# A decoder layer on one Trainium2 core: norms of heads taken for two tiles of tokens together, values third among the projections, and a filler's pace set by its present steps

## The chip, the cores and the metric

The kernel is one program on one core of a Trainium2 chip. The metric is device time in microseconds (us). Before the change three runs took 2496.92, 2497.53 and 2503.78 us; their median is 2497.53.

The core has a matrix engine (TensorE, PE in the profile, with its weight loads listed as PEld), a vector engine (VectorE, DVE), a scalar engine (ScalarE, ACT), and queues of transfers. In this kernel every transfer is issued by SyncE (SP), in the order of its instructions. Matrix products land in PSUM, which has eight banks of 128 x 512 numbers; a tile there may take one bank or two.

## The reference, cut to what matters

One layer of a decoder on 1024 tokens of width 1024: a half-step feed-forward, a mixing part with three kinds of attention, and a second half-step. The change lies in the mixing part:

```
u  = rmsnorm(h)
(fq, fk, fv, ff, dq, dk, dv, iq, ik, iw, mq, g) = split(u @ w_in)
fq, fk = rmsnorm per head (8 heads of 64);  o_a = forgetting attention(fq, fk, fv, log_sigmoid(ff))
dq     = rope(rmsnorm per head (8 heads of 64)); iq, ik = rope(...)
o_b    = attention of dq over the 256 keys with the highest sum_h iw_h * relu(iq_h . ik)
mq     = rmsnorm per head (4 heads of 128);  o_c = attention of mq into 256 memory tokens
h      = h + (sum_i sigmoid(g_i) * (o_i @ w_branch_i)) @ w_out
```

## The kernel before, in words

Tokens are taken in eight tiles of 128. Each product of float32 numbers is done in three passes: operands are split into a high and a low part (`wH`, `wL` for weights; the cast to `wH` is on ScalarE, the difference `wL` on VectorE), so that 8 slices of the inner size 1024 make 24 matmuls for one tile of 128 tokens and 512 columns.

The stages follow one another: first feed-forward up to about 706 us of the span, norms and narrow projections, then the *projections* up to about 1118 us, the *heads* up to about 1697 us (four memory heads, eight forgetting heads, eight sparse heads, two at a time), the *last branch* up to 1757 us, the output product up to 1840 us, and the second feed-forward.

**Projections.** Six blocks of 512 columns, listed in `blocks` (line 1675): memory queries, index queries, forget keys, forget queries, values, sparse queries. A block has eight steps, one for each tile: `Block.step` (line 353) takes one PSUM bank (`bank("tm")`), issues the 24 matmuls, asks for the next block's weights in its last step, and hands the tile to a `consume` function. For keys and queries this is a norm by head (`head_norm`, line 857): a square on ScalarE (`hsq<-tm`), a sum by head on VectorE (`hv<-hsq`), nine small steps of VectorE for the inverse root (`rsqrt_mean`: `hv`, `rs_y`, `rs_a`), and a multiply that reads the bank again (`hsq<-tm,rs_y`). Then `turn` transposes the tile on TensorE (`turn<-ident,hsq`), splits it (`th`, `tl`), and the halves are stored. For sparse queries a rotation on VectorE stands between norm and `turn`. Values (`fox_values`) are only split and stored; their tile has the tag `iqs`, with two buffers.

Index queries go further: for tiles 2 to 7 the queries are loaded back (also under the tag `iqs`, two buffers), and for each of eight heads TensorE computes scores against the keys (`isc`, into a two-bank tile `banks2("isc")`), ScalarE takes the relu in place, and VectorE adds them up (`acc`). A background chain then looks for the 256th highest score of each token by a binary search (`junk` on ScalarE, `sk` and `sn` on VectorE).

While projections run, PSUM is cut into four single banks (tag `a`, used by `bank`) and two double ones (tag `b`, used by `banks2`).

**What sets the order.** The work is written as chains (generators), and a planner, `_Flow.run`, steps them at build time: it charges estimated costs to each engine, and picks the first of the `width` oldest chains that is ready by TensorE's clock, else a step of a filler (12 matmuls of the gate products `gate`), else it waits. The framework afterwards reorders instructions on each engine by its own estimates, so the order on an engine is finer than the planner's steps.

**Heads and their filler.** During the heads the filler (`fill`, line 1697) has the remaining gate steps, then 16 steps of one branch product (memory), four steps that wait for forgetting heads, and 17 of another. `pace` (line 1754) lets it run while its count of steps is below a share of `left` that grows with the heads' steps, plus 4, and below `left` − 6. `left` is gate steps remaining + 40. After the heads the last branch (sparse, `last_branch`) starts, once the filler is done; its first operands are the heads' outputs (`o_s`) and the weights `in_w_branch`.

Of the kernel before, what the change touches and what calls it, by code (L numbers as in the profile page):

```python
# [9 lines left out]
F32 = mybir.dt.float32  # L10
# [9 lines left out]
P = 128  # L20
# [11 lines left out]
C_FQ, C_FK, C_FV, C_FF = 0, 512, 1024, 1536  # L32
C_DQ, C_DK, C_IQ, C_IK, C_MQ, C_G = 1544, 2056, 2184, 2696, 2768, 3280
# [122 lines left out]
def trunk_layer_kernel(  # L156
# [6 lines left out]
    fl = _Flow(nc)  # L163
    T, A, V = fl.T, fl.A, fl.V
    chain = _Chain
# [3 lines left out]
    def plain(ap):  # L169
        return ap.bitcast(F32) if ap.dtype == F32R else ap  # L170
# [4 lines left out]
    def store(o, i):  # L175
        nc.sync.dma_start(plain(o), plain(i))
# [19 lines left out]
    def pool(name, bufs=1, **kw):  # L196
        return Pool(name, bufs, **kw)
# [18 lines left out]
    def bank(name="bank"):  # L216
        return banks["pool"].tile([P, 512], F32, tag="a", name=name, bufs=banks["single"])
# [4 lines left out]
    def banks2(name="banks2"):  # L222
        return banks["pool"].tile([P, 1024], F32, tag="b", name=name, bufs=2)
# [6 lines left out]
    def split(high, low, v):  # L230
        A.copy(high, v)
        V.tensor_sub(low, v, high.bitcast(F32))
# [101 lines left out]
    def mm3(pt, terms, first, last, onto=False):  # L334
        n = len(terms)
        for i, (a, b) in enumerate(terms):
            T.matmul(pt, a, b, start=first and i == 0, stop=last and i == n - 1, skip_group_check=onto)

    class Block:
# [13 lines left out]
        def step(self, u, t, consume, after=None):  # L353
            self.fetch()
            if fl.clk["PE"] < self.ready[0]:
                yield self.ready[0]
            if after is not None:
                after.fetch(self.bufs - len(self.srcs))
            pt = self.out(t) if self.out else bank("tm")
            kper = 1024 // self.ncols  # L360
            for k in range(NK):
                wh, wl = self.ws[k // kper]
                wh, wl = wh[:, k % kper], wl[:, k % kper]
                a, b = [u.at(w, k, t * P, P) for w in range(2)]
                mm3(pt[:, :self.ncols], [(a, wh), (a, wl), (b, wh)], k == 0, k == NK - 1)
                if after is not None and k % kper == kper - 1:
                    after.fetch(self.bufs - len(self.srcs) + k // kper + 1)
            yield from consume(t, pt)

    def col_srcs(w, c0, ncols):  # L370
        kper = 1024 // ncols
# [5 lines left out]
    def block_chains(blocks, u, nt, deps=None, after=None):  # L377
        cs = []
        for i, (b, consume) in enumerate(blocks):
            nxt = blocks[i + 1][0] if i + 1 < len(blocks) else after  # L380
            order = getattr(consume, "order", range(getattr(consume, "first", 0), nt))
            for t in order:
                cs.append(chain(b.step(u, t, consume, nxt if t == order[-1] else None),
                                deps[t] if deps and i == 0 else getattr(consume, "deps", ())))
        return cs

# [81 lines left out]
    class FeedForward:  # L468
# [62 lines left out]
        def product(self, pt, j, n, start):  # L531
            sh, sl = self.jobs[j][n]
            th, tl = self.c.high[RIGHT[n]], self.c.low[RIGHT[n]]
            for k in range(4):
                mm3(pt, [(sh[:, k], th[:, k]), (sh[:, k], tl[:, k]), (sl[:, k], th[:, k])],
                    start and k == 0, k == 3, not start)
# [64 lines left out]
        def first_half(self, beside=None):  # L601
# [10 lines left out]
            def prep(g, *js):  # L612
                for j in js:
                    if g in (1, 2):
                        self.prep_sums(j, g - 1)
                    self.prep_split(j, g)

            step()
            c.split(T2, 2)
            prep(1, 0, 1)  # L620
# [212 lines left out]
    def scratch(name, shape):  # L833
        return dram.tile(shape, F32, name=name)
# [3 lines left out]
    fq_s = scratch("fq_s", [2, 8, 64, S])  # L838
    fk_s = scratch("fk_s", [2, 8, 64, S])
    dq_s = scratch("dq_s", [2, 8, 64, S])  # L840
# [3 lines left out]
    mq_s = scratch("mq_s", [2, 4, P, S])  # L844
# [10 lines left out]


    def head_norm(tp, pt, nh, sq=None):
        hd = 512 // nh
        if sq is None:
            sq = tp.tile([P, 512], F32, tag="hx", name="hsq", bufs=4)  # L860
        A.activation(sq, pt, AF.Square)
        v = tp.tile([P, nh], F32, tag="hv", name="hv", bufs=3)
        V.reduce_sum(v, sq.rearrange("p (h d) -> p h d", h=nh), axis=AX.X)
        y = rsqrt_mean(tp, v, hd)
        V.tensor_tensor(
            sq.rearrange("p (h d) -> p h d", h=nh), pt.rearrange("p (h d) -> p h d", h=nh),
            y.unsqueeze(2).to_broadcast([P, nh, hd]), op=OP.mult,
        )
        return sq


    def turn(tp, xn, scale=None):
        pt = bank("turn")
        for j in range(4):
            T.transpose(pt[:, j * P:(j + 1) * P], xn[:, j * P:(j + 1) * P], ident)
        th = tp.tile([P, 4, P], F32R, tag="th", name="th", bufs=2)
        tl = tp.tile([P, 4, P], F32R, tag="tl", name="tl", bufs=2)
        thf, tlf = th.rearrange("p a t -> p (a t)"), tl.rearrange("p a t -> p (a t)")
        if scale is None:
            split(thf, tlf, pt)  # L880
        else:
            A.activation(thf, pt, AF.Identity, scale=scale)
            V.scalar_tensor_tensor(tlf, pt, scale, thf.bitcast(F32), op0=OP.mult, op1=OP.subtract)
        return th, tl

    def store_pairs(dst, t, parts):
        for i, th in enumerate(parts):
            store(dst[i].rearrange("(a b) d t -> (b d) a t", b=2)[:, :, t * P:(t + 1) * P], th)
# [115 lines left out]
    def rotate(tp, o, xv, cv, sv0, sv1, n, op1=OP.add):  # L1004
        t2 = tp.tile([P, n, 2, 32], F32, tag="hx", name="rot2", bufs=4)
        V.tensor_tensor(o, xv, cv, op=OP.mult)
        V.tensor_tensor(t2[:, :, 0], xv[:, :, 1], sv0, op=OP.mult)
        V.tensor_tensor(t2[:, :, 1], xv[:, :, 0], sv1, op=OP.mult)
        if op1 == OP.add:
            V.tensor_add(o, o, t2)  # L1010
        else:
            V.tensor_sub(o[:, :, 0], o[:, :, 0], t2[:, :, 0])
            V.tensor_add(o[:, :, 1], o[:, :, 1], t2[:, :, 1])
# [397 lines left out]
    gfx, gfk, gmx, gmk = [vec.tile([P, 1], F32, name=n) for n in ("gfx", "gfk", "gmx", "gmk")]  # L1411
# [79 lines left out]
    up, u = mixing["up"], mixing["u"]  # L1491
# [5 lines left out]
    gates_f = chain(gates.work())  # L1497
    norms = [chain(to_mix(t)) for t in range(4, NT)]
    nch = block_chains([(nb, narrow)], u, NT, [[]] * 4 + [[c] for c in norms])
    order = norms[:1] + nch[:2] + norms[1:2] + nch[2:3] + norms[2:3] + nch[3:4] + norms[3:]  # L1500
# [8 lines left out]
    tp = pool("proj")  # L1509
    tmp = pool("narrow")  # L1510
    cs, sn = tp.tile([P, NT, 32], F32, name="rope_cos"), tp.tile([P, NT, 32], F32, name="rope_sin")
    cgq, sgq = [tp.tile([P, NT, 2, 32], F32, name=n) for n in ("cgq", "sgq")]
# [3 lines left out]
    mk_block = lambda c0: Block(blk, col_srcs(w_in, c0, 512), 512, 5)  # L1516
    mq_block = mk_block(C_MQ)
# [126 lines left out]
    index_queries.first, index_queries.deps = 2, [prep]  # L1644
    sel_c = chain(selection())

    def normed(dst, nh, scale):
        def consume(t, pt):
            xn = head_norm(tp, pt, nh)
            yield  # L1650
            parts = turn(tp, xn, scale)
            if nh == 8:
                store_pairs(dst, t, parts)
            else:
                for i, w in enumerate(parts):
                    store(dst[i].rearrange("h d t -> d h t")[:, :, t * P:(t + 1) * P], w)
        return consume

    def sparse_queries(t, pt):
        xn = head_norm(tp, pt, 8)  # L1660
        o = tp.tile([P, 512], F32, tag="hx", name="hsq", bufs=4)
        bc = lambda a, s: a.unsqueeze(1).to_broadcast(s)
        rotate(tp, o.rearrange("p (h a d) -> p h a d", h=8, a=2), xn.rearrange("p (h a d) -> p h a d", h=8, a=2),
               bc(cgq[:, t], [P, 8, 2, 32]), bc(sgq[:, t, 0], [P, 8, 32]), bc(sgq[:, t, 1], [P, 8, 32]), 8)
        yield
        store_pairs(dq_s, t, turn(tp, o))

    def fox_values(t, pt):
        vt = tp.tile([P, 8, P], F32R, tag="iqs", name="iqs", bufs=2)
# [2 lines left out]
        return  # L1672
        yield

    blocks = [(mq_block, normed(mq_s, 4, gmx[:, 0:1])), (mk_block(C_IQ), index_queries),
              (mk_block(C_FK), normed(fk_s, 8, None)), (mk_block(C_FQ), normed(fq_s, 8, gfx[:, 0:1])),
              (mk_block(C_FV), fox_values), (mk_block(C_DQ), sparse_queries)]
    chains = block_chains(blocks, u, NT)
    fl.run(chains[:2] + [prep] + chains[2:], width=5, filler=gates_f, background=sel_c, margin=0.5)
    tp.release()  # L1680
# [6 lines left out]
    tp = pool("att")  # L1687
# [60 lines left out]
    sparses = [chain(sparse_chain(i)) for i in range(8)]  # L1748
    fill_c = chain(fill())
    heads = mems + foxes + sparses  # L1750
    left = 2 * 24 * 2 - gates_f.n + 40
    total = 4 * 10 + 8 * 16 + 8 * 20

    def pace():
# [27 lines left out]
    hp = pool("h2", side="right")  # L1782
    h = [hp.tile([P, D], F32, name=f"h2_{t}") for t in range(NT)]
    for t in range(NT):
        load(h[t], h_s[t])
    tp = pool("norm3", side="right")
# [34 lines left out]
    blocks = [(Block(None, col_srcs(w_out, i * 512, 512), 512, 4), f) for i, f in enumerate((residual, normed_rows))]  # L1821
# [51 lines left out]
```

## Time and profile before

| | |
|---|---|
| median of three runs | 2497.53 us |
| the profiled execution's own time | 2504.25 us |
| its span | 2502.2 us |
| granted TensorE clock, mean over the span | 0.984 |
| bytes moved | 352.15 MB, 141 GB/s |

The profile is one execution; times within it are from the start of the span. Each row of the views has an engine, an operation, and its tiles as out<-in, by the names used above. "Idle before" is the time for which the engine stood still just ahead of these instructions, with what released it. Matmul ends are modelled, so a matmul's own duration (about 0.39 us) is longer than the distance between the starts of two. The number after the clock is the share of the DMA engines that was busy.

### The profile page before, as it was taken

What the parts mean: (1) busy time and instruction counts of PE and PEld (TensorE: products, weight loads), DVE (VectorE), ACT (ScalarE), POOL (GpSimd) and SP (SyncE); (2) the same over time, 40 slices, a digit from 0 to 9 for tenths busy, and PEclk for the clock granted to TensorE, in tenths of its full rate; (3) what the DMA queues carried; (4) which work ended last, traced back from release to release, by engine and by line L of the source; (5) the groups of instructions that cost most, each with busy time, mean ns of one, the idle gap of its engine ahead of it and who ended that gap; (6) DMA issues with size and microseconds to landing.
All of it is one profiled execution on the core that took longest, in us unless ns stands there. A gap on an engine that the chain in (4) does not pass through costs nothing.

```text
span 2502.2 us, 31494 instructions
## 1 busy us (share of the span) xinstructions
PE 2412.6 (96%) x11532; PEld 1995.0 (80%) x11532; DVE 1617.9 (65%) x3162; ACT 1149.1 (46%) x1918; POOL 2.2 (0%) x40
## 2 busy tenths in 40 slices
PE   6999999999999999989999999998999999999999
PEld 5888888888788877777787888887877888888887
DVE  7755555478767588685564556777367555554885
ACT  6443333343443376768864555543144333333332
POOL 0000000000000000000000000000000000000000
PEclk8999999999999999999999999999999999999999
DMA  4333322484445534544554546667413222225643
GB/s 136 117 103 110 101 92 73 146 316 142 135 131 146 163 100 137 164 147 137 153 162 135 154 133 195 194 200 238 145 64 93 85 93 76 84 93 194 260 151 131
DMA packets 300922, 352.15 MB, mean 141 GB/s; under 512 B 19896, under 2 KB 202840, under 8 KB 300768
## 3 DMA queue, kind: packets, MB, share of 16 engines
q1 hardware_dynamic: 300768, 350.15, 43.7%
q8 instruction: 90, 1.47, 0.2%
q14 instruction: 64, 0.52, 0.1%
HBM read 255.51 MB, written 93.54 MB: 139 GB/s over the span
## 4 chain that ended last, share of the span: by engine, by line
PE 74%; DVE 12%; ACT 7%; DMA 4%; issue 3%; SPq 0%; ACTq 0%; DVEq 0%
PE gx L51 19%; PE gy L51 14%; PE dx L51 8%; PE gate L51 7%; PE tm L51 7%; PE dy L51 6%; PE br L51 4%; ACT junk L51 3%; PE po L51 2%; PE sp L51 2%; DVE wL L51 2%; PE pT L51 2%; DMA wS<-in_ffn_w_down 1%; PE nar L51 1%; ACT ns L51 1%
## 5 line engine op out<-in xcount | busy, mean ns | idle before, releaser
L51 ACT CAST wH<-wS 128x1024 fp32r<-128x1024 f32 (+1 forms) x218 | 204.6, 944 | 260.7 <-PE gy L51 78.0
L51 PE MATMUL tm<-wH,u 128*128 128x512 f32 x992 | 319.5, 396 | 3.4 <-ACT wH L51 3.4
L51 DVE TENSOR_TENSOR wL<-wS,wH 128x1024 fp32r<-128x1024 f32 (+1 forms) x218 | 236.2, 1089 | 101.1 <-ACT wH L51 98.8
L51 PE MATMUL gate<-u,wH 128*128 128x512 f32 x768 | 248.9, 401 | 0.0
L51 PE MATMUL gx<-th,wH 128*128 128x512 f32 x704 | 223.2, 399 | 10.3 <-ACT wH L51 6.2
L51 PE MATMUL gy<-th,wH 128*128 128x512 f32 x704 | 220.9, 395 | 5.3 <-DVE th L51 3.5
L51 PEld LDWEIGHTS tm<-wH,u 128*128 128x128 f32 x992 | 187.4, 189 | 42.0 <-ACT wH L51 4.6
L51 PE MATMUL gx<-raw,wH 128*128 128x512 f32 x704 | 216.9, 389 | 0.4 <-DVE gu L51 0.4
L51 PE MATMUL tm<-wL,u 128*128 128x512 f32 x496 | 195.1, 393 | 1.0 <-DVE wL L51 0.8
L51 ACT ACTIVATE junk<-wk,sn 128x384 bf16<-128x384 f32 (+5 forms) x186 | 164.3, 883 | 67.4 <-DVE sn L51 59.0
L51 PEld LDWEIGHTS gx<-th,wH 128*128 128x128 f32 x704 | 135.0, 193 | 40.6 <-ACT wH L51 7.4
L51 ACT CAST wH<-S 128x1024 fp32r<-128x1024 f32 x88 | 92.2, 1051 | 157.9 <-PE gy L51 149.9
L51 PEld LDWEIGHTS gy<-th,wH 128*128 128x128 f32 x704 | 133.6, 190 | 34.7 <-DVE th L51 4.4
L51 PEld LDWEIGHTS gate<-u,wH 128*128 128x128 f32 x768 | 140.3, 191 | 24.8 <-DVE u L51 0.2
L51 DVE TENSOR_TENSOR pl<-pT,ph 128x512 fp32r<-128x512 f32 (+1 forms) x176 | 110.1, 639 | 74.5 <-ACT ph L51 73.1
L51 DVE TENSOR_TENSOR wL<-S,wH 128x1024 fp32r<-128x1024 f32 x88 | 107.4, 1223 | 75.1 <-ACT wH L51 75.1
L51 DVE TENSOR_TENSOR gu<-gu,gy 128x512 f32<-128x512 f32 x88 | 60.3, 686 | 147.0 <-PE gy L51 104.1
L51 PEld LDWEIGHTS gx<-raw,wH 128*128 128x128 f32 x704 | 132.0, 188 | 28.2 <-DVE gu L51 0.8
L51 PE MATMUL gate<-u,wL 128*128 128x512 f32 x384 | 151.7, 395 | 0.0
L51 PE MATMUL dx<-wH 128*128 128x512 f32 x352 | 138.4, 393 | 2.7 <-DVE rows L51 2.6
L51 PE MATMUL gx<-th,wL 128*128 128x512 f32 x352 | 139.1, 396 | 0.6 <-DVE wL L51 0.5
L51 PE MATMUL gy<-th,wL 128*128 128x512 f32 x352 | 138.8, 394 | 0.0
(270 smaller groups left out, 5018.1 us busy)
## 6 DMA issues: line engine op xcount, KB each, us to landing
wS<-in_ffn_w_down SPq DMA_DIRECT2D x70, 512.0 KB
wS<-in_w_in SPq DMA_DIRECT2D x48, 512.0 KB
wS<-in_ffn_w_gate SPq DMA_DIRECT2D x46, 512.0 KB
wS<-in_ffn_w_up SPq DMA_DIRECT2D x44, 512.0 KB
hid_s<-gu SPq DMA_DIRECT2D x44, 512.0 KB
a<-hid_s SPq DMA_DIRECT2D x30, 512.0 KB
g_s<-sg SPq DMA_DIRECT2D x48, 256.0 KB
bg<-g_s SPq DMA_DIRECT2D x48, 256.0 KB
```

The costliest lines, as they stand in the source:

```text
L51: return fn(*a, **k)
```

## The change

1. `Block.pair` computes tiles t and t+1 of a block one after the other into one two-bank tile, `banks2("tm")`, and hands both to `consume` at once. Forget keys, forget queries and sparse queries use it; the norm is then taken once for 16 heads in 1024 columns (`hsq` of 128 x 1024, a tag of its own, `hp`, with two buffers). Transposes and stores stay per tile. Memory queries stay single.
2. Values come third in `blocks`, ahead of forget keys.
3. `left` is gate steps remaining + 37, which is the number of steps that the filler has (16 + 4 + 17).

```
-            pt = self.out(t) if self.out else bank("tm")
...
+        def pair(self, u, t, consume, after=None):
...
+            pt = banks2("tm")
+            self.product(pt[:, :512], u, t, None)
+            yield 0.0
+            if after is not None:
+                after.fetch(self.bufs - len(self.srcs))
+            self.product(pt[:, 512:], u, t + 1, after)
+            yield from consume(t, pt)
...
+    def pair_norm(pt):
+        return head_norm(tp, pt, 16, tp.tile([P, 1024], F32, tag="hp", name="hsq", bufs=2))
+
+    def normed_pair(dst, scale):
         def consume(t, pt):
...
+            xn = pair_norm(pt)
+            for i in range(2):
+                yield
+                store_pairs(dst, t + i, turn(tp, xn[:, i * 512:(i + 1) * 512], scale))
+        return in_pairs(consume)
...
+    @in_pairs
+    def sparse_queries(t0, pt):
+        xn = pair_norm(pt)
...
+        os_ = []
+        for i in range(2):
...
+            os_.append((o, fl.t))
+        for i in range(2):
+            yield max(os_[i][1], fl.t if i else 0.0)
+            store_pairs(dq_s, t0 + i, turn(tp, os_[i][0]))
...
-    blocks = [(mq_block, normed(mq_s, 4, gmx[:, 0:1])), (mk_block(C_IQ), index_queries),
-              (mk_block(C_FK), normed(fk_s, 8, None)), (mk_block(C_FQ), normed(fq_s, 8, gfx[:, 0:1])),
-              (mk_block(C_FV), fox_values), (mk_block(C_DQ), sparse_queries)]
+    blocks = [(mq_block, memory_queries), (mk_block(C_IQ), index_queries), (mk_block(C_FV), fox_values),
+              (mk_block(C_FK), normed_pair(fk_s, None)), (mk_block(C_FQ), normed_pair(fq_s, gfx[:, 0:1])),
+              (mk_block(C_DQ), sparse_queries)]
...
-    left = 2 * 24 * 2 - gates_f.n + 40
+    left = 2 * 24 * 2 - gates_f.n + 37
```

TensorE has the same 11532 matmuls before and after; their order differs. On TensorE, in the midst of the index scores, before (`isc` are scores, `gate` is the filler; `ikk` and `iqs` are the index keys and queries):

```order
L51 MATMUL gate<-u_4704,wH 128x512
L51 MATMUL gate<-u_4704,wL 128x512
L51 MATMUL gate<-u_4704,wH 128x512 x2
L51 MATMUL gate<-u_4704,wL 128x512
L51 MATMUL isc<-ikk_5380,iqs 128x512
L51 MATMUL isc<-ikk_5381,iqs 128x512
L51 MATMUL isc<-ikk_5380,iqs 128x512
L51 MATMUL isc<-ikk_5381,iqs 128x512
L51 MATMUL gate<-u_4704,wH 128x512
```

The same place after the change, where the last product ahead of the first pair ends (`tm` is a projection's product):

```order
L51 MATMUL tm<-wH,u_4704 128x512 x2
L51 MATMUL tm<-wL,u_4704 128x512
L51 MATMUL tm<-wH,u_4704 128x512
L51 MATMUL isc<-ikk_5380,iqs 128x512
L51 MATMUL isc<-ikk_5381,iqs 128x512
L51 MATMUL isc<-ikk_5380,iqs 128x512
L51 MATMUL isc<-ikk_5381,iqs 128x512
L51 MATMUL isc<-ikk_5380,iqs 128x512
L51 MATMUL isc<-ikk_5381,iqs 128x512
L51 MATMUL isc<-ikk_5380,iqs 128x384
L51 MATMUL isc<-ikk_5381,iqs 128x384
```

Before, scores of one or two heads alternate with products and gate steps. After, 28 score matmuls (seven heads) stand in a row, of which eight are shown; the next row is the first product of a pair. Six more heads' scores come after that.

On SP's queue, at the end of the heads, before (`wS` are weights on their way in, or the heads' outputs from `o_s`; `mg_s` are the merged branches, stored and loaded again as `bm`; `bg` are the gates):

```order
L173 DMA oR<-r_s 64x1024
L173 DMA wS<-o_s 128x1024
L176 DMA mg_s<-bg 128x512
L173 DMA wS<-in_w_branch 128x4x256
L176 DMA mg_s<-bg 128x512
L173 DMA wS<-in_w_branch 128x4x256 x2
L173 DMA bg<-g_s 128x512
```

And after:

```order
L173 DMA wS<-o_s 128x1024
L176 DMA mg_s<-bg 128x512
L173 DMA bg<-g_s 128x512
L173 DMA bm<-mg_s 128x512
L176 DMA mg_s<-bg 128x512
L173 DMA bg<-g_s 128x512
L173 DMA wS<-in_w_branch 128x4x256
L176 DMA mg_s<-bg 128x512
L173 DMA wS<-in_w_branch 128x4x256
L176 DMA mg_s<-bg 128x512
L173 DMA wS<-in_w_branch 128x4x256
```

The first load of `in_w_branch` has moved behind one more store and three loads, and each later one behind a store of its own; each of these stores writes the result of one step of the filler. After the last head 60 matmuls of the filler (five steps) are left ahead of the last branch, where there were 24 (two steps).

More of the change, by code (lines that the diff above doesn't have):

```diff
@@ L359, in step, with product @@
             pt = self.out(t) if self.out else bank("tm")
+            self.product(pt, u, t, after)
+            yield from consume(t, pt)
+        def pair(self, u, t, consume, after=None):
+            self.fetch()
+            if fl.clk["PE"] < self.ready[0]:
+                yield self.ready[0]
+            pt = banks2("tm")
[4 more added lines that the diff above has]
+            self.product(pt[:, 512:], u, t + 1, after)
+            yield from consume(t, pt)
+        def product(self, pt, u, t, after):
             kper = 1024 // self.ncols
@@ L367, in step @@
                     after.fetch(self.bufs - len(self.srcs) + k // kper + 1)
-            yield from consume(t, pt)
     def col_srcs(w, c0, ncols):
@@ L380, in block_chains @@
             nxt = blocks[i + 1][0] if i + 1 < len(blocks) else after
-            order = getattr(consume, "order", range(getattr(consume, "first", 0), nt))
+            pair = getattr(consume, "pair", False)
+            order = range(getattr(consume, "first", 0), nt, 2 if pair else 1)
             for t in order:
-                cs.append(chain(b.step(u, t, consume, nxt if t == order[-1] else None),
+                cs.append(chain((b.pair if pair else b.step)(u, t, consume, nxt if t == order[-1] else None),
                                 deps[t] if deps and i == 0 else getattr(consume, "deps", ())))
@@ L857, in head_norm @@
     def head_norm(tp, pt, nh, sq=None):
-        hd = 512 // nh
+        hd = pt.shape[-1] // nh
         if sq is None:
@@ L1645, in trunk_layer_kernel, with in_pairs, memory_queries @@
     sel_c = chain(selection())
-    def normed(dst, nh, scale):
-        def consume(t, pt):
[L1649 to L1661, printed above, removed]
-        bc = lambda a, s: a.unsqueeze(1).to_broadcast(s)
[L1663 to L1666, printed above, removed]
+    def in_pairs(consume):
+        consume.pair = True
+        return consume
+    def pair_norm(pt):
+        return head_norm(tp, pt, 16, tp.tile([P, 1024], F32, tag="hp", name="hsq", bufs=2))
+    def normed_pair(dst, scale):
+        def consume(t, pt):
+            xn = pair_norm(pt)
[3 more added lines that the diff above has]
+        return in_pairs(consume)
+    def memory_queries(t, pt):
+        xn = head_norm(tp, pt, 4)
+        yield
+        for i, w in enumerate(turn(tp, xn, gmx[:, 0:1])):
+            store(mq_s[i].rearrange("h d t -> d h t")[:, :, t * P:(t + 1) * P], w)
+    @in_pairs
+    def sparse_queries(t0, pt):
+        xn = pair_norm(pt)
+        bc = lambda a, s: a.unsqueeze(1).to_broadcast(s)
+        os_ = []
+        for i in range(2):
+            t = t0 + i
+            o = tp.tile([P, 512], F32, tag="hx", name="hsq", bufs=4)
+            rotate(tp, o.rearrange("p (h a d) -> p h a d", h=8, a=2),
+                   xn[:, i * 512:(i + 1) * 512].rearrange("p (h a d) -> p h a d", h=8, a=2),
+                   bc(cgq[:, t], [P, 8, 2, 32]), bc(sgq[:, t, 0], [P, 8, 32]), bc(sgq[:, t, 1], [P, 8, 32]), 8)
+            os_.append((o, fl.t))
+        for i in range(2):
+            yield max(os_[i][1], fl.t if i else 0.0)
+            store_pairs(dq_s, t0 + i, turn(tp, os_[i][0]))
     def fox_values(t, pt):
```

## The prediction

> **What bounds the kernel now.** I began with the page: the share of each engine, the granted clock, and the chain that ended last.
>
> ```profile
> span 2502.2 us, 31494 instructions
> ...
> PE 2412.6 (96%) x11532; PEld 1995.0 (80%) x11532; DVE 1617.9 (65%) x3162; ACT 1149.1 (46%) x1918; POOL 2.2 (0%) x40
> ...
> PEclk8999999999999999999999999999999999999999
> ...
> PE 74%; DVE 12%; ACT 7%; DMA 4%; issue 3%; SPq 0%; ACTq 0%; DVEq 0%
> ```
>
> TensorE is busy for 96% of the span. A change that leaves every matmul in place, as this one does, can only touch the rest: waits of TensorE and the stretches of lowered clock behind them. So the next view was busy time by stage: projections, their end, heads, the tail of the heads, and the last branch.
>
> ```profile
> core 0: us, PE busy (x) PEld busy (x) DVE busy (x) ACT busy (x) POOL busy (x), PEclk, DMA share, GB/s
> 838.00:1108.00 270.00, 257.73 (x1170) 208.02 (x1168) 213.70 (x718) 188.83 (x382) 0.00 (x0) 0.98 0.44 131
> 1108.00:1126.00 18.00, 10.38 (x45) 8.48 (x46) 11.53 (x41) 10.89 (x23) 0.00 (x0) 0.82 0.91 308
> 1126.00:1697.00 571.00, 552.77 (x3189) 465.14 (x3188) 360.87 (x895) 346.55 (x719) 0.00 (x0) 0.99 0.54 161
> 1697.00:1720.00 23.00, 16.14 (x62) 12.43 (x62) 13.20 (x17) 6.63 (x8) 0.00 (x0) 0.78 0.71 245
> 1720.00:1760.00 40.00, 40.00 (x178) 33.14 (x177) 33.03 (x49) 12.84 (x18) 0.00 (x0) 1.00 0.77 256
> ```
>
> The projections leave TensorE idle for 270.00 − 257.73 = 12.3 us, their end 7.6, the heads 18.2, the tail 6.9. The last row is TensorE at its own pace: 40.00 / 178 = 0.225 us a matmul, so 24 matmuls (one tile of tokens) take 5.4 us and a gate or branch step of 12 takes 2.7. What ended the idle times is in TensorE's waits, first from 838 to 1126 us, then in the tail:
>
> ```profile
> PE spm L51 <- DMA km<-km_s: 7.4, 2, 4.5
> PE turn L51 <- DVE hsq L51: 3.9, 2, 3.0
> PE isc L51 <- DVE acc L51: 3.8, 3, 1.9
> PE tm L51 <- ACT wH L51: 2.5, 1, 2.5
> ```
>
> ```profile
> PE br L51 <- ACT wH L51: 6.6, 1, 6.6
> ```
>
> The columns are total, number, longest. The norms are late for TensorE only twice ("turn" behind "hsq", 3.9 us). All they can win is there.
>
> **The clock.** A wait costs more than itself, as three short windows show:
>
> ```profile
> 922.00:926.00 4.00, 2.08 (x11) 1.45 (x10) 4.00 (x15) 1.57 (x4) 0.00 (x0) 1.00 0.37 110
> 943.00:951.00 8.00, 6.73 (x24) 5.47 (x25) 7.79 (x19) 5.69 (x10) 0.00 (x0) 0.79 0.61 180
> 996.00:1001.00 5.00, 3.77 (x13) 3.25 (x14) 4.41 (x23) 4.15 (x9) 0.00 (x0) 0.66 0.50 160
> 1057.00:1062.00 5.00, 4.97 (x15) 3.83 (x16) 3.40 (x7) 4.01 (x7) 0.00 (x0) 0.66 0.95 280
> ```
>
> The first holds 1.9 us of idle time and kept its clock (1.00). The second holds 1.3 and ran at 0.79 over 8 us; the last two stand at the ends of the 3.0 us wait for "hsq" and the 2.5 us wait for "wH", and ran at 0.66 over 5. Each loses the same: 0.21 × 8 or 0.34 × 5 = 1.7 us of work. So a wait of 2 to 3 us costs 1.7 us more, sometimes.
>
> The Trainium skill (TensorE: Matmul & The Clock Gate, "HAM oscillation — how this bites in real kernels") puts the limit at idle gaps over some 3.4 us. The trace disagrees in part: shorter gaps here had a lowered clock behind them, and one of 1.9 us had none.
>
> **The change, part by part.** Durations in the projection stage (last columns: busy us, mean ns):
>
> ```profile
> L51 DVE TENSOR_TENSOR wL<-wS,wH 128x1024 fp32r<-128x1024 f32 x27 | 33.1, 1224 | 7.5 <-ACT wH L51 7.1
> L51 ACT CAST wH<-wS 128x1024 fp32r<-128x1024 f32 x27 | 28.2, 1047 | 13.0 <-DMA wS<-in_w_in 7.0 <-PE gate L51 4.0 <-PE tm L51 2.1
> L51 DVE TENSOR_REDUCE hv<-hsq 128x8 f32<-128x512 f32 (+1 forms) x33 | 22.6, 684 | 12.1 <-ACT hsq L51 10.8
> L51 DVE TENSOR_TENSOR hsq<-tm,rs_y 128x512 f32<-128x512 f32 x32 | 22.1, 690 | 0.5
> L51 ACT ACTIVATE hsq<-tm 128x512 f32<-128x512 f32 x32 | 18.9, 589 | 37.7 <-PE tm L51 34.4 <-DVE sk L51 3.2
> L51 DVE SCALAR_TENSOR_TENSOR rs_y<-rs_a,rs_y 128x8 f32<-128x8 f32 (+1 forms) x66 | 10.8, 164 | 1.3
> ```
>
> *Norms in pairs.* 24 of 32 norms become 12. Each saves nine small VectorE steps of about 0.164 us: 12 × 9 × 0.164 = 17.7 us of VectorE. That engine has 56 us free in the 270, and TensorE waited for a norm only for 3.9 us, so nearly all of it lies beside other work. On the path it takes away the 3.9 and the 1.7 of lowered clock at 997, of which I count 1.1 because TensorE was idle in part of that window: **−5**. The reverse is possible too: a pair's norm is longer, with 1024 columns by about 1.05 (square), 1.22 (reduce), nine times 0.164 and 1.22 us (multiply), 4.9 us against 3.4 (a tile of 1024 columns taken at the 1.05 and 1.22 us of the first two rows); but it has 48 matmuls, 10.8 us, of the next pair to hide under.
>
> *Values third.* The block whose weight was late at 1057 (2.5 us, with a window of lowered clock, 4.2 in all) is reached in another way. I keep about 1 us for the transitions of the blocks: **−3**, bounds −4.2 and 0. But the values' tiles carry the tag of the scores' operands ("iqs", two buffers). Now the scores' load of tile 7 waits for a store of values, and VectorE gets values' work while it still adds up scores. Nearest rows are the waits of the scores for "acc", up to 1.9: **+2.5**, bounds 0 and 5.
>
> *Pairs against scores for the two double banks.* A pair takes one of the two double banks, where before every product took a single one and the scores had both. The order in front shows the outcome: the first pair of forget keys stands behind 28 score matmuls, seven heads, with nothing else between; before, products and gate work stood between. What heads in a row cost can be read where two stood close:
>
> ```profile
> 939.97 1.07 PE L51 MATMUL isc<-ikk,iqs 128*128 128x512 f32 x4
> ...
> 941.11 0.96 PE L51 MATMUL isc<-ikk,iqs 128*128 128x512 f32 x4
> ...
> 941.67 1.80 ACT L51 ACTIVATE isc<-isc 128x1024 f32<-128x1024 f32 x2
> ...
> 942.94 2.34 DVE L51 SCALAR_TENSOR_TENSOR acc<-isc,iw,acc 128x1024 f32<-128x1024 f32 x2
> ...
> 944.27 0.50 PE L51 MATMUL isc<-ikk,iqs 128*128 128x512 f32 x1 [1.74 <-DVE acc L51]
> ```
>
> Two heads from 939.97 let the next begin at 944.27: 4.3 us a pair of heads, with one "wL" of 1.2 us between. At that rate the last of seven heads starts after 13 us (6 × 2.15), and TensorE has worked 28 × 0.225 = 6 of them at most: **+7**, bounds +2 (no weights split beside them: 1.17 us of "acc" a head, seven times, against 6) and +9. The old waits of scores for "acc" (3.8 us, and part of the window at 943) go with the old interleaving; a little stays: **−3**.
>
> After the burst six heads and two more pair starts share what a pair leaves: one double bank. Each start needs a head's relu and add (0.90 + 1.17) or the norm of the pair before (nearly 5) to end, with 0.7 to 5.4 us of products to cover it. Worked through row by row I get waits of 2.1, 3.4, 3.5 and 0.8, 9.8 in all; since the compiler's clock is not the chip's, I take **+7**, bounds 3 and 10. New waits of 2 to 3.5 us bring lowered clock, two windows of 1.7: **+3**, bounds 0 and 5.
>
> The Trainium skill (TensorE: Matmul & The Clock Gate, "A second HAM failure mode: psum-queue depth-cycling") speaks against this change: cycling through banks leaves TensorE small idle times between groups, and the clock oscillates. By that sentence each of the seven heads would bring a window, an estimate of +12 instead of +3; the row of 922 to 926, a wait for a bank at a clock of 1.00, speaks against so much.
>
> *End of the stage.* Queries of the sparse heads end in a pair, so both rotations come before the last turns; the load of "km" still stands behind their last store on SP's queue:
>
> ```profile
> 1111.48 0.36 SPq L176 DMA_DIRECT2D dq_s<-tl  x1
> ...
> 1112.94 0.42 SPq L173 DMA_DIRECT2D km<-km_s  x1
> ```
>
> TensorE waited 7.4 us for "km". One rotation is made of these:
>
> ```profile
> L51 DVE TENSOR_TENSOR rot<-hsq,sgq 128x256 f32<-128x256 f32 x16 | 6.0, 418 | 0.0
> L51 DVE TENSOR_TENSOR hsq<-hsq,cgq 128x512 f32<-128x512 f32 x8 | 5.5, 691 | 0.1
> L51 DVE TENSOR_TENSOR hsq<-hsq,rot 128x512 f32<-128x512 f32 x8 | 5.5, 691 | 0.0
> ```
>
> That is 0.69 + 2 × 0.42 + 0.69 = 2.2 us. After, the last turns wait for the pair's norm and both rotations, 4.9 + 4.4 = 9.3 us, with 24 gate matmuls (5.4) as cover: 3.9 us of waiting. The stores then leave by as much later as the cover moved, so of the 7.4 I keep 5 to 6: about 9.4 against 7.4 and 1 of small waits, **+1**, bounds −2 and +3.
>
> *Pace.* `left` is 37 for 40, so three filler steps (3 × 2.7 = 8.1 us) pass from the heads to the tail: 60 filler matmuls stand there for 24. In the heads they covered waits: all 8.1 come back if other heads cover them, none if not; the stage has only 18.2 idle of 571. I take **−4**. In the tail TensorE works 8.1 longer before the last branch. Its weights' loads now stand on SP's queue behind stores that wait for those steps:
>
> ```profile
> 1702.21 0.35 SPq L173 DMA_DIRECT2D wS<-o_s  x1
> ...
> 1703.08 0.43 SPq L173 DMA_DIRECT2D wS<-in_w_branch  x1
> ...
> 1705.65 1.10 SPq L173 DMA_DIRECT2D wS<-in_w_branch  x2
> ```
>
> ```profile
> 1710.38 1.22 PE L51 MATMUL br<-o,wH 128*128 128x512 f32 x2 [6.63 <-ACT wH L51]
> ```
>
> Before, the load was issued at 1703.08 and the 6.6 us wait ended 7.3 us later at 1710.38. After, it follows the third step, about 10.5 us into the filler, so the wait is 10.5 + 7.3 − 13.5 = 4.3 instead of 6.6. The lowered clock behind it (1 − 0.78 = 0.22 of 23 us, 5.1) shrinks to one window of 1.7. Tail: 8.1 − 2.3 − 3.4 = **+2.4**, bounds −1 and +6.
>
> **Sum.** −5 − 3 + 2.5 + 7 − 3 + 7 + 3 + 1 − 4 + 2.4 = +7.9 us. The profiled execution took 2504.25 us, 2.05 of them around its span, so it would take 2512.2. It lies 6.7 above the median of the runs, 2497.53; a difference carries over, so the forecast is **2505.5**.
>
> **Rivals.** (1) *The scores run at their own pace* (no change): with no norm in flight during the burst, VectorE has only "acc" to do, 1.17 us a head, and the pair starts behind it find their bank free. For it: the wait at 922 cost no clock. Burst +2, single bank +3, no windows: 2505.5 − 5 − 4 − 3 = 2493.5. Against it: weights are split in just that stretch. (2) *The tail decides, the kernel is faster.* Place: heads and last branch. The steps leave the heads for nothing (−8.1 for −4) and fully cover the load, as the load goes out earlier than I think (tail 0): another −4.1 − 2.4 = −6.5 on rival 1: 2487. It decides from the point where TensorE's wait before the last branch is below 2 us. Against it: the stores ahead of the load in the new order. (3) *The clock decides*, the rule above as a mechanism of this kernel: lowered clock after each head of the burst and each pair start, seven windows for two, 5 × 1.7 = 8.5 more: 2514. For it: 943 and 996. That the pairing does nothing is hardly possible: 108 small steps are gone from VectorE's order. But that it has no path to shorten is my forecast's first step.
>
> **Chances.** Forecast 0.42, rival 1 0.23, rival 2 0.18, rival 3 0.17. About 0.3%, 7.5 us, is what a measurement here tells from no change, so the bounds are 2490 and 2505. The forecast lies on the upper one: of its 0.42 I put 0.28 above and 0.14 within; rival 1 lies within, rival 2 below, rival 3 above. Faster 0.18, same 0.37, slower 0.45. The range leaves out half of rival 2 and part of rival 3: 2485 to 2516. The forecast's own range, without rival 2, would be 2493 to 2516.
>
> **What would show it.** Right: in the projections' first 100 us after the keys' start, TensorE waits of "isc" and "tm" for "acc" or "isc" of 10 us or more; no "turn" behind "hsq" before the last pair; a wait of "br" for "wH" of 3 to 6 us. Wrong: TensorE's idle time from the first score to the first "spm" no longer than now (12.3 + 7.6 us), or a last branch that starts without a wait.

## The result and the profile after

The changed kernel takes 2526.67 us (median of four runs, 2524.93 to 2527.66), against 2498.04 for the kernel before: a ratio of 1.0109, 95% interval 1.0092 to 1.0127. It is slower by 28.6 us where 7.9 had been forecast, and outside the range, which ended at 2516. The profiled execution took 2527.22 us. Its page:

```profile
span 2525.2 us, 31338 instructions
...
PE 2418.2 (96%) x11532; PEld 1996.8 (79%) x11532; DVE 1605.1 (64%) x3030; ACT 1148.5 (45%) x1906; POOL 2.2 (0%) x40
...
PE 71%; DVE 12%; ACT 7%; DMA 7%; issue 3%; SPq 1%; ACTq 0%; DVEq 0%
```

The matmuls are the same 11532. VectorE has 132 instructions and 12.8 us less to do, and the kernel is 23 us longer by its span. Where they went, by stages that begin and end at the same work (first score to first memory score, then to the end of the heads, then to the end of the last branch), first of the kernel before, then of the changed one (columns as in the windows above: length, busy time of TensorE, its weight loads, VectorE, ScalarE and GpSimd, granted clock, DMA share, GB/s):

```profile
838.00:1119.00 281.00, 264.02 (x1200) 213.07 (x1199) 223.19 (x747) 194.15 (x393) 0.00 (x0) 0.98 0.46 137
1119.00:1698.00 579.00, 557.85 (x3211) 469.46 (x3210) 363.84 (x907) 352.52 (x731) 0.00 (x0) 0.99 0.54 164
...
1698.00:1757.00 59.00, 52.14 (x218) 42.17 (x217) 42.69 (x59) 17.67 (x24) 0.00 (x0) 0.91 0.78 265
```

```profile
835.00:1133.00 298.00, 269.28 (x1199) 214.50 (x1197) 210.47 (x620) 195.68 (x386) 0.00 (x0) 0.97 0.42 128
1133.00:1715.00 582.00, 553.21 (x3179) 465.82 (x3180) 359.89 (x897) 349.82 (x726) 0.00 (x0) 0.98 0.52 159
...
1715.00:1779.00 64.00, 59.05 (x251) 48.27 (x250) 44.38 (x61) 16.77 (x22) 0.00 (x0) 0.95 0.81 269
```

From 281 to 298 in the projections, from 579 to 582 in the heads although 32 recorded matmuls left them, from 59 to 64 in the tail. Taken exactly, from the first and last matmuls, these are 280.7 to 297.8 (+17.1), 579.5 to 581.7 (+2.2) and 58.9 to 64.4 (+5.5); the rest of the span is 1.8 us shorter. Of TensorE's waits from 830 to 1140 us these are the longest groups:

```profile
PE isc L51 <- DVE acc L51: 6.7, 3, 2.9
PE turn L51 <- DVE hsq L51: 5.7, 2, 4.5
PE tm L51 <- DVE acc L51: 5.1, 2, 2.7
PE spm L51 <- DMA km<-km_s: 5.0, 2, 2.8
PE isc L51 <- DVE sk L51: 3.2, 4, 1.2
PE turn L51 <- DVE sk L51: 2.2, 3, 1.3
PE isc L51 <- DMA iqs<-iq_s: 1.9, 3, 1.1
PE turn L51 <- DVE sn L51: 1.1, 1, 1.1
```

Scores wait for a double bank to be added up ("isc" behind "acc", 3.8 before), pairs' products wait for the same ("tm" behind "acc", not there before), and transposes wait for VectorE as before, under more names. The burst of scores looks like this:

```profile
929.45 1.80 ACT L51 ACTIVATE isc<-isc 128x1024 f32<-128x1024 f32 x2
...
930.48 1.28 DVE L51 TENSOR_SCALAR acc<-isc,iw 128x1024 f32<-128x1024 f32 x1 [0.56 <-ACT isc L51]
931.68 1.14 DVE L51 SCALAR_TENSOR_TENSOR acc<-isc,iw,acc 128x896 f32<-128x896 f32 x1
...
931.82 2.75 PE L51 MATMUL isc<-ikk,iqs 128*128 128x512 f32 x8 [2.86 <-DVE acc L51]
...
935.07 2.34 DVE L51 SCALAR_TENSOR_TENSOR acc<-isc,iw,acc 128x1024 f32<-128x1024 f32 x2
936.40 3.06 PEld L51 LDWEIGHTS isc<-ikk,iqs 128*128 128x128 f32 x8 [2.33 <-DVE acc L51]
936.40 3.57 PE L51 MATMUL isc<-ikk,iqs 128*128 128x512 f32 x8 [1.83 <-DVE acc L51]
```

Two heads start at 931.82 and the next two at 936.40: 4.6 us for two heads, where TensorE stands still for 2.86 and then 1.83 us. From here to the last wait of a pair's product, which ends at 981.37, the granted clock is 0.84:

```profile
931.00:985.00 54.00, 42.63 (x158) 32.31 (x159) 36.96 (x101) 35.39 (x68) 0.00 (x0) 0.84 0.29 93
```

### The profile page after: what moved, and what is told of

The parts are those of the page before. It is cut to its first block, busy times and chain, and to the rows that moved or that the text cites. A ratio compares the mean times of both kernels' runs of the same rounds, so it can differ in the third digit from the quotient of the medians.

```text
span 2525.2 us, 31338 instructions
## 1 busy us (share of the span) xinstructions
PE 2418.2 (96%) x11532; PEld 1996.8 (79%) x11532; DVE 1605.1 (64%) x3030; ACT 1148.5 (45%) x1906; POOL 2.2 (0%) x40
## 4 chain that ended last, share of the span: by engine, by line
PE 71%; DVE 12%; ACT 7%; DMA 7%; issue 3%; SPq 1%; ACTq 0%; DVEq 0%
PE gx L51 18%; PE gy L51 14%; PE gate L51 7%; PE dx L51 7%; PE tm L51 6%; PE dy L51 6%; ACT junk L51 3%; PE po L51 2%; DVE wL L51 2%; PE pT L51 2%; PE sp L51 2%; PE br L51 2%; DMA wS<-in_ffn_w_down 2%; DVE acc L51 1%; PE nar L51 1%
## 5 line engine op out<-in xcount | busy, mean ns | idle before, releaser
L51 DVE TENSOR_TENSOR wL<-S,wH 128x1024 fp32r<-128x1024 f32 x88 | 107.4, 1223 | 73.9 <-ACT wH L51 73.9
L51 PE MATMUL dx<-wL,wH 128*128 128x512 f32 x352 | 138.1, 392 | 0.3 <-DVE wL L51 0.3
```

Of the source, the lines that this page charges most:

```text
L51: return fn(*a, **k)
```

## The experiments

Theory A: a pair of products takes a two-bank tile that the index scores need, and TensorE waits. Its rivals: B, values third is what costs; C, the pace is. Later runs part A into A1, the two-bank tile, and A2, the longer chain of the joint norm. Each run is compared with runs of the kernel before on the same chip (medians of 2497.9 to 2500.5 us); ratios stand with their 95% interval, and 0.001 is 2.5 us. A change to the kernel also shifts the planner's order, so no run differs from another in one wait alone.

**Pace alone.** The kernel before with one line changed:

```
-    left = 2 * 24 * 2 - gates_f.n + 40
+    left = 2 * 24 * 2 - gates_f.n + 37
```

> The kernel before with left at 37 for 40 and nothing else. Theory A (pairs of products take a double PSUM bank from the index scores, and the projections pay for it): this kernel has no pairs, the projections take 280.7 us from the first score to the first memory score as before, and the time is 2494 to 2501. Theory B (values third is what costs): the same, 2494 to 2501. Theory C (the pace costs, since the last branch's weights now stand behind the filler's stores and the heads lose cover): 2504 to 2510, most of it between the first memory score and the last branch.

Measured: 2507.67 us, 1.0032 [1.0020, 1.0045]. C holds, with about 8 us. The heads and one wait in them:

```profile
1116.00:1696.00 580.00, 552.36 (x3176) 464.78 (x3177) 361.46 (x906) 353.27 (x734) 0.00 (x0) 0.98 0.51 160
```

```profile
PE sp L51 <- DMA ks<-fk_s: 4.6, 1, 4.6
```

35 matmuls have left the heads for the tail (TensorE 557.85 to 552.36 us busy), and the heads last 580 as before. A forgetting head now waits 4.6 us for its keys, which it did not before. The changed kernel has the same wait:

```profile
PE sp L51 <- DMA ks<-fk_s: 4.8, 1, 4.8
```

**Pace the other way.** The kernel before with 42 for 40.

> The kernel before with left at 42 for 40: more filler in the heads, one step of it instead of two left for the tail. Theory D (the heads last some 580 us whatever filler they get, since the filler only covers their waits): first memory score to the end of the heads 576 to 584 us, the tail shorter by 2.7 us of products but with a longer wait of br for its weights: 2492 to 2500. Against it: the heads grow by the 5.4 us that they get more, 2499 to 2506.

Measured: 2510.17 us, 1.0037 [1.0024, 1.0049]. Theory D falls: the heads last 590 us, 11 more and not only the 5.4 that they got in matmuls, and the tail's wait grows too.

```profile
1118.00:1708.00 590.00, 565.47 (x3235) 475.31 (x3235) 367.98 (x916) 353.62 (x732) 0.00 (x0) 0.98 0.54 164
```

```profile
PE br L51 <- ACT wH L51: 11.8, 2, 11.3
```

So 40 lies between two slower values, and the heads' length does not follow from the amount of filler in either direction.

**Values third alone.** The kernel before with this list:

```
-              (mk_block(C_FK), ...), (mk_block(C_FQ), ...), (mk_block(C_FV), fox_values), (mk_block(C_DQ), ...)]
+              (mk_block(C_FV), fox_values), (mk_block(C_FK), ...), (mk_block(C_FQ), ...), (mk_block(C_DQ), ...)]
```

> The kernel before with values third and single products throughout, left at 40. Theory A: no pair takes a double bank, the scores flow, 2496 to 2503. Theory B (values' tiles share two buffers with the scores' operands and values load VectorE while scores are added up): 2510 or more, with the first score to the first memory score at 290 us or more. Theory C: as before, 2495 to 2500.

Measured: 2503.83 us, 1.0020 [1.0009, 1.0032]: 5 us, between A and B. One wait of TensorE stands out (last row), and VectorE's rows before it tell why:

```profile
1045.91 1.48 DVE L51 TENSOR_TENSOR_SCAN wk<-one,sq 128x640 f32<-128x640 f32 x1
...
1047.37 1.22 DVE L51 TENSOR_TENSOR wL<-wS,wH 128x1024 fp32r<-128x1024 f32 x1
...
1048.59 1.22 DVE L51 TENSOR_TENSOR wL<-wS,wH 128x1024 fp32r<-128x1024 f32 x1
...
1052.41 0.68 DVE L51 TENSOR_TENSOR hsq<-tm,rs_y 128x512 f32<-128x512 f32 x1
...
1053.23 1.09 PE L51 MATMUL turn<-ident,hsq 128*128 128x128 f32 x4 [6.11 <-DVE one L51]
```

The norm's multiply came at 1052.41 because its small steps stood in VectorE's queue among a scan of the search and two weight splits; the transpose behind it waited 6.1 us.

**Pairs alone.** The changed kernel with values fifth and left at 40.

> The changed kernel with values fifth again and left at 40, so pairs alone. Theory A: the projections lose as much as in the changed kernel, 12 to 20 us, 2508 to 2520. Theory B: the gain of the norms stays and the loss goes, 2490 to 2500. Theory C: 2495 to 2500.

Measured: 2553.37 us, 1.0216 [1.0202, 1.0230]: 54 us, nearly twice the whole change, and beyond what A had expected. Values third hide part of what pairs do: in this run four pairs reach their norm among the scores (squares at 902, 925, 952 and 976 us), in the changed kernel two (958 and 977). The stretch of the scores in this run, and its waits from 830 to 1180 us:

```profile
837.00:1000.00 163.00, 133.41 (x529) 104.38 (x528) 108.27 (x300) 102.19 (x211) 0.00 (x0) 0.83 0.33 100
```

```profile
PE isc L51 <- DVE acc L51: 15.1, 8, 2.4
PE isc L51 <- DMA iqs<-iq_s: 5.7, 1, 5.7
PE tm L51 <- DVE acc L51: 5.6, 2, 3.2
PE isc L51 <- DVE sk L51: 4.3, 6, 1.1
```

163 us from first to last score, against 125.0 before. The clock is 0.83 over the whole stretch: 0.17 x 163 = 28 us, nearly as much again as TensorE's idle time of 29.6. A part of it follows the one long wait, 5.7 us for "iqs" up to 875 us. But from 900 us on no wait is longer than 2.4 us, and the clock is as low:

```profile
900.00:1000.00 100.00, 79.59 (x305) 61.29 (x304) 67.35 (x203) 63.65 (x129) 0.00 (x0) 0.83 0.31 93
```

Another 16 us are lost between the last score and the first memory score (171.8 for 155.7 before); 5.4 of these are 24 gate matmuls that have come over from the heads.

**Pairs and pace.** The changed kernel with values fifth.

> The changed kernel with values fifth again, so pairs and pace. Theory A: nearly all of the change stays, 2518 to 2528. Theory B: 2498 to 2506. Theory C: the tail's and the heads' part stays, some 8 us, 2503 to 2508. If parts only add, its distance from the run with pairs alone is that of the pace alone from the kernel before.

Measured: 2547.17 us, 1.0192 [1.0178, 1.0206], above the ranges of all three theories. The parts don't add: with pairs ahead of it the pace takes some 6 us off (the intervals just overlap; the heads last 567 us for 581), alone it adds 8. What the pace does depends on the order that it meets.

**Products in pairs, norms apart.** The changed kernel; in the code only the norm differs:

```
     def pair_norm(pt):
-        return head_norm(tp, pt, 16, tp.tile([P, 1024], F32, tag="hp", name="hsq", bufs=2))
+        xn = tp.tile([P, 1024], F32, tag="hp", name="hsq", bufs=2)
+        for i in range(2):
+            head_norm(tp, pt[:, i * 512:(i + 1) * 512], 8, xn[:, i * 512:(i + 1) * 512])
+        return xn
```

> The changed kernel with the pairs' products as they are, in one two-bank tile, but a norm for each half, as before. Theory A1 (the two-bank tile that a pair takes from the scores is the cost): the loss stays, 2522 to 2535, since only small VectorE steps come back. Theory A2 (the longer chain of the joint norm holds TensorE up): the loss of the projections goes, 2506 to 2515.

Measured: 2526.60 us, 1.0102 [1.0085, 1.0118], the changed kernel's time. The range of A1, and A2 falls: the joint norm, the point of the change, is worth nothing that can be told in the time. The stages shift all the same (projections 300.5 us for 297.8, with 24 gate matmuls more in them; heads 579.0 for 581.7). The run leaves the pairing of the products as the cost, but it does not tell the two-bank tile from the order in which a pair's products stand.

**Norms together, products in single banks.** The changed kernel; the pair takes `bank("tm")` twice, and squares and multiplies go half by half around one sum and one root:

```
-            pt = banks2("tm")
-            self.product(pt[:, :512], u, t, None)
+            pt = bank("tm")
+            self.product(pt, u, t, None)
...
-            self.product(pt[:, 512:], u, t + 1, after)
-            yield from consume(t, pt)
+            pt2 = bank("tm")
+            self.product(pt2, u, t + 1, after)
+            yield from consume(t, (pt, pt2))
```

> The changed kernel with the joint norm as it is, but each of a pair's two products in a single bank of its own, so that the scores keep both double banks. Theory A1: the projections (first score to first memory score) come down from 298 us to 280 to 286, and the time to 2508 to 2516; what stays is the pace. Theory A2: 2522 to 2530.

Measured: 2521.79 us, 1.0084 [1.0068, 1.0101]. Just below the range of A2, whose cause the run before rules out, and only 5 us of the 11 to 19 that A1 expected: from first to last score 133.1 us instead of 142.5, but afterwards products wait for a single bank that a transpose holds, and the projections come down by only 3.7, to 294.1:

```profile
PE tm L51 <- DVE tl L51: 7.2, 2, 4.6
```

**The same with values fifth and left at 40**, beside the run with pairs alone.

> As the run with pairs alone (values fifth, left 40, 2553), but each product in a single bank and only the norm joint. Theory A1: the 55 us go, 2492 to 2503. Theory A2: most of them stay, 2535 or more. In between if TensorE now lacks single banks, with waits of products for hsq.

Measured: 2524.53 us, 1.0087 [1.0063, 1.0111]: 29 us of the 54 go, between the two ranges; one product waits 2.0 us for "hsq" there. The scores' stretch gives back more than that, 42 us: it is at 121 us with no lowered clock, and the waits of scores for "acc" up to 1000 us are down to 1.7 from 15.1 in all (those for "sk" stay, 4.0 for 4.3):

```profile
837.00:958.00 121.00, 114.54 (x530) 90.58 (x529) 94.24 (x244) 85.52 (x173) 0.00 (x0) 1.00 0.44 130
```

```profile
PE isc L51 <- DVE acc L51: 1.7, 1, 1.7
```

This is the clearest sign for A1, in the scores' stretch. What stays, 22 us, lies behind the scores and does not go with the banks: 172.6 us from the last score to the first memory score, as with pairs alone, and the heads last 590 us for 579, at a clock of 0.97 for 0.99.

**Three double banks.** The changed kernel with PSUM cut into two single and three double banks in the projections.

> The changed kernel with PSUM cut into two single and three double banks during the projections, instead of four and two, so that a pair leaves two double banks to the scores. Theory A1: the waits of scores for acc fall, the time is 2510 to 2520, unless two single banks are too few for products, turns and gate steps; then 2530 or more, with waits of tm, turn and gate for single banks in place of the old ones.

Measured: 2544.25 us, 1.0175 [1.0160, 1.0189]. From the first score to the first memory score it takes 289.2 us for 297.8, and scores wait 1.7 for "acc" instead of 6.7, as A1 says; those for "sk" and "iqs" make 7.0 for 5.1, so that all waits of scores come to 8.7 for 11.8. But the first score starts at 858.6 instead of 835.3: with two single banks, products of the first blocks wait for them, from 706 to 860 us among others like this:

```profile
PE tm L51 <- DVE tl L51: 8.9, 6, 1.7
```

**No pairs.** The kernel before with values third and left at 37.

> The changed kernel without its pairs: values third and left at 37, with single products and a norm for each tile. If the parts add, 2498 + 6 + 10 = 2514, and pairs cost 13 us in the changed kernel (55 alone). Theory A1: between 2506 and 2518. Against it: 2522 or more, so that pairs cost nothing once values stand third.

Measured: 2515.51 us, 1.0055 [1.0042, 1.0067]. Values and pace add (0.0020 + 0.0032 = 0.0052), and with them in place pairs cost the rest, 1.0109 for 1.0055: 13 us.

**Which pairs.** The changed kernel with forget keys single; then with forget queries single as well (pairs for sparse queries only); then with sparse queries single and the other two in pairs. Theory E says that pairs of sparse queries, which end the stage, are what costs beside the scores; theory F says that pairs of forget queries are.

> The changed kernel with forget keys single; forget queries and sparse queries stay in pairs. Theory A1: the pairs no longer meet the scores, so this is the run without pairs within 4 us, near 2514. Theory A3 (pairs also cost after the scores, as the run with late pairs suggests, since a turn stands behind the longer norm and the search's small steps on VectorE): 2520 to 2530.

> The changed kernel with forget keys and forget queries single, so pairs for sparse queries only. It lies between the run without pairs (2515.5) and the run with forget keys single (2520.4). Theory E: at the second, 2519 to 2524. Theory F: at the first, 2512 to 2517.

> The changed kernel with sparse queries single, so pairs for forget keys and forget queries. Theory E: the end of the stage goes back to 1.0 and 7.4 us of waits, and 3 to 6 us of the changed kernel's time go, 2520 to 2524. Theory F: 2524 to 2530.

Measured: 2520.41 us, 1.0083 [1.0068, 1.0099]; 2515.31 us, 1.0061 [1.0041, 1.0081]; 2525.98 us, 1.0109 [1.0091, 1.0126]. The first lies at the lower edge of A3's range, beyond A1's 4 us; the other two lie in the ranges of F. So in the changed kernel pairs of sparse queries cost nothing that can be told (theory F), pairs of forget queries about 5 us, pairs of forget keys about 6. The intervals overlap, so the last two are sizes, not verdicts.

**Late pairs with values fifth and left at 40**: forget queries and sparse queries, then sparse queries alone.

> Pairs in two-bank tiles for forget queries and sparse queries only; forget keys, which stand among the scores, are single; values fifth, left 40. Theory A1: no pair meets a score, 2488 to 2500, with no wait of scores beyond those of the kernel before. Theory A2: the joint norms of 8 of 12 pairs still cost, 2510 or more.

> Pairs for sparse queries only; forget keys and queries single, values fifth, left 40. Theory E (a pair that ends the stage holds the last turns and the first memory head, and 24 gate matmuls pass from the heads into the projections to cover it, without making the heads shorter): most of the 23 us of the run with late pairs is here, 2512 to 2524. Theory F (the pairs of forget queries are what costs there): 2497 to 2504.

Measured: 2522.89 us, 1.0093 [1.0068, 1.0119], and 2510.05 us, 1.0044 [1.0029, 1.0059]. Both are slower than A1 expected, and the second lies between the ranges of E and F. Pairs that come when the scores are nearly done still cost. That their norms are what costs, as A2 has it, does not fit the run with norms apart. With pairs for sparse queries alone a part can be read:

```profile
836.00:1127.00 291.00, 270.96 (x1221) 219.04 (x1219) 218.80 (x702) 194.08 (x389) 0.00 (x0) 0.98 0.44 132
1127.00:1707.00 580.00, 553.37 (x3187) 466.65 (x3187) 363.70 (x908) 351.68 (x731) 0.00 (x0) 0.98 0.54 163
```

```profile
PE turn L51 <- DVE sn L51: 4.7, 1, 4.7
```

Some 24 gate matmuls (5.4 us) have moved from the heads into the projections to cover the last pair, a turn still waits 4.7 us there, and the heads last 580 us without them. That is theory E's mechanism in this order of blocks, but only 10 of the 23 us; in the changed kernel, where the count of gate matmuls ahead of the heads is that of before, E fails.

No version that I ran beats the kernel before. What the background search does to these waits was not tried.

## Why the prediction was wrong

By the profiles the forecast of +7.9 was made of +9.5 for the projections, −4 for the heads and +2.4 for the tail. Measured: +17.1, +2.2 and +5.5. Another 5.6 us is the base, the step "a difference carries over": the profiled execution of before lay 6.2 us above the median that its runs now have, that of after 0.6. Some of it can be seen: over the first 100 us, which the change doesn't touch, the granted clock was 0.90 before and is 0.95 after:

```profile
0.00:100.00 100.00, 77.76 (x328) 61.77 (x329) 78.41 (x121) 57.44 (x81) 1.08 (x8) 0.90 0.39 122
```

```profile
0.00:100.00 100.00, 77.25 (x333) 61.32 (x334) 78.32 (x121) 58.01 (x82) 1.08 (x8) 0.95 0.40 125
```

The first feed-forward ended 2.4 us later in the execution of before (705.85 for 703.43). A difference of two profiles has such errors. 17.1 + 2.2 + 5.5 − 1.8 + 5.6 gives the 28.6.

Of the 17.1 us of the projections, waits make 11.7 (TensorE idle for 298.00 − 269.28 = 28.7 us, before 281.00 − 264.02 = 17.0), and lowered clock most of the rest (read in slices of some 40 us, it takes 10.4 us of work after and 4.8 before).

*Right, and about right in size.* The burst (+7): TensorE stands still for 2.86, 1.83 and 0.92 us in it, 5.6. One double bank beside the pairs (+7): "tm" behind "acc" 5.1 in two waits and one of "isc" of 2.0, 7.1. The old waits of scores (−3): their 3.8 are gone. The weight's wait at 1057 (−3): gone. The end of the stage (+1): 4.5 and 5.0 of waits for 1.0 and 7.4. All of this is theory A, and the runs with single banks and with three double ones bear it out: they bring the waits for "acc" down. Rival 1 falls with the burst, and rival 2 with the wait before the last branch, 4.95 us where it needed less than 2. Two of the three signs of being right came ("isc" and "tm" wait 11.8 us for "acc", 4.7 of it in the burst just ahead of the first pair; the wait of "br" is 4.95); the third did not, since one "turn" still waits 1.1 us for "hsq" before the last pair.

*Wrong: "On the path it takes away the 3.9 and the 1.7 of lowered clock at 997", the term −5.* Leaving out the end of the stage, transposes wait in the projections for VectorE 1.2 + 2.2 + 1.1 = 4.5 us after, against 3.9 before. The wait was not the norm's own length alone; it was the norm's place in VectorE's queue, behind steps of the search, a transpose's "tl" and weight splits. The 3.0 us wait of before shows it:

```profile
991.28 0.68 DVE L51 TENSOR_REDUCE hv<-hsq 128x8 f32<-128x512 f32 x1
...
992.66 1.22 DVE L51 TENSOR_TENSOR_SCAN wk<-one,sq 128x512 f32<-128x512 f32 x1
...
996.39 0.69 DVE L51 TENSOR_TENSOR hsq<-tm,rs_y 128x512 f32<-128x512 f32 x1
```

From the start of the sum to the end of the multiply 5.8 us pass, of which the norm's own steps take some 2.9 (0.68 + 9 x 0.164 + 0.69). A longer step in the same queue waits as well. The run with norms apart agrees: the joint norm does not change the time. Of the 17.7 us that VectorE was to save, the page shows 12.8.

*Wrong in size: the clock (+3).* Two windows of 1.7 had been forecast. From 931 to 985 us the clock is 0.84, which is 0.16 x 54 = 8.6 us of work, as much as five such windows. The windows at 943, 997 and 1057 that went do not make up for it.

*Wrong in size: values third (+2.5).* Alone the step costs 5 us, and in the changed kernel "isc" waits 3.2 for "sk" and 1.9 for "iqs"; without the 0.92 that stands in the burst these are 4.2. I had looked for the shared buffers and found them; the queue of VectorE was again what I left out.

*Wrong: "all 8.1 come back if other heads cover them, none if not; I take −4".* None came back. TensorE's idle time in the heads grew from 579.00 − 557.85 = 21.2 to 582.00 − 553.21 = 28.8 us, about what the moved matmuls had filled (35 x 0.225 = 7.9), and a wait of 4.6 to 4.8 us for a head's keys was new. With the pace alone the heads last 580 us for 579. The two runs on either side of 40 show that this part doesn't follow from amounts: the heads are 20 chains in an order that shifts with each count, and keys are loaded on one queue behind other heads' stores. In the changed kernel the loads of keys ahead of the 4.8 us wait's end (1233.30) leave from 1227.63 on, behind a store of "o_s" at 1226.37 and one of "r_s" at 1226.78.

*Wrong in size: the tail (+2.4).* Its load is issued, and the wait ends, here:

```profile
1726.94 0.43 SPq L173 DMA_DIRECT2D wS<-in_w_branch  x1
...
1733.27 2.93 PE L51 MATMUL br<-o,wH 128*128 128x512 f32 x6 [4.95 <-ACT wH L51]
```

The load leaves 12.1 us after the heads' end (1714.85), not 10.5; the wait is 4.95, not 4.3; and 3.2 us of lowered clock stay (0.05 x 64), where 1.7 had been expected.

Rival 3, the clock, said 2514 by seven windows for two. The changed kernel has as much as five of them, and much more is seen in the run with pairs alone. The Trainium skill (TensorE: Matmul & The Clock Gate, "A second HAM failure mode: psum-queue depth-cycling") says that small idle times between groups of matmuls, as banks are cycled through, make the clock go down and up. That trace agrees: waits of at most 2.4 us and a clock of 0.83 from 900 to 1000 us. The Trainium skill's limit of some 3.4 us for a single gap (the same page, "HAM oscillation — how this bites in real kernels") does not hold in that stretch.

What stays open: why pairs of forget queries cost about 5 us in the changed kernel, and the late pairs 23 with values fifth. Of the 23, the sparse queries' gate steps explain a part, and the heads another: they last 586 us at a clock of 0.97 there, for 579 at 0.99 before, though only 24 gate matmuls have left them. Open too is how much of the pairs' 13 us in the changed kernel is the two-bank tile, since single banks give back only 5 and bring waits of their own. Waits there are spread over "turn", "tm" and "wL" at 1 to 3 us each, and no run of mine takes one alone away.

## What to carry to other kernels

Fewer instructions on an engine that is not the bound are worth only the waits that they end. Here a wait came from what stood ahead in VectorE's queue, and fewer small steps of one norm did not end it. Ask what a merge takes in return: here it took a two-bank tile for an estimated 16 us (48 matmuls of 0.225 and a norm of 4.9) from the one stage that lives on two of them, and the clock then charged for many of the small waits again. Where a planner orders the work, undo each part alone on the chip before adding up: the same three steps of pace cost 8 us in one order and gained some 6 in another.

## What the runs showed of the hardware

Doubling the width did not double the step, yet it was far from free: the norm's three wide steps in the changed kernel took 1013, 1219 and 1223 ns for 589, 684 and 690 at half the width, and a small step of 16 columns 175 for 164 at eight (rows of the projections, mean ns after the busy time).

```profile
L51 ACT ACTIVATE hsq<-tm 128x1024 f32<-128x1024 f32 x12 | 12.2, 1013 | 1.8 <-PE tm L51 1.7
L51 DVE TENSOR_REDUCE hv<-hsq 128x16 f32<-128x1024 f32 x12 | 14.6, 1219 | 6.0 <-ACT hsq L51 6.0
L51 DVE TENSOR_TENSOR hsq<-tm,rs_y 128x1024 f32<-128x1024 f32 x12 | 14.7, 1223 | 0.1
L51 DVE SCALAR_TENSOR_TENSOR rs_y<-rs_a,rs_y 128x16 f32<-128x16 f32 x24 | 4.2, 175 | 0.5
```

And the granted clock can stay low over 100 us (0.83 from 900 to 1000 us with pairs alone) without one wait of TensorE above 2.4 us in them.
